# Layer 0's attention in float32 on half-array tiles of TensorE, in place of two fp32r parts

## The chip, the cores and the metric

The program runs on one core of one Trainium2 chip. The metric is the device time of one execution in microseconds (us). TensorE (PE) multiplies; VectorE (DVE), ScalarE (ACT) and GpSimd (POOL) do the rest on data in on-chip memory; SyncE (SP) issues most DMAs. An engine runs its own list of instructions in order. A `matmul` is a weight load (of the stationary operand, PEld in the profile) and a stream of the moving operand's columns (PE in the profile) into PSUM.

## The reference, cut to what matters

A two-layer transformer block on 512 latent tokens and 256 context tokens, width 1024, heads of 64. Layer 0's mixer is grouped attention, 4 query heads for each of 4 key/value heads: heads 0 and 1 (of the four) see the context and a window of 128 tokens to either side, with a sink; heads 2 and 3 see all tokens.

```python
qa = _rms(qa.reshape(b, n, HEADS_A, d), qn_a)      # the same for ka, qb, kb
qa, ka, qb, kb = _rope(qa, cos, sin), ...          # latent tokens only
...
s_c = jnp.einsum('bqhgd,bkhd->bhgqk', qb, k_ctx).astype(jnp.float32) * scale
s_w = jnp.einsum('bqhgd,bkhd->bhgqk', qb, kw).astype(jnp.float32) * scale
s_w = jnp.where(ok, s_w, NEG_INF)
p = _softmax(jnp.concatenate([s_c, s_w], axis=-1), sink_b).astype(v_lat.dtype)
return (jnp.einsum('bhgqk,bkhd->bqhgd', p[..., :n_ctx], v_ctx)
        + jnp.einsum('bhgqk,bkhd->bqhgd', p[..., n_ctx:], vw))
```

The output projection, a SwiGLU FFN, and layer 1 (differential attention, FFN) follow. All of it is float32.

## The kernel before

Tokens lie in 6 tiles of 128: tiles 0 to 3 are latent, 4 and 5 the context, which comes first in most loops (`CTX_FIRST`). A float32 product is made of fp32r ones: each operand is split into `hi` (a cast to fp32r) and `lo` (the rest), and three products are summed, or two where one operand's two parts lie side by side on the array.

Layer 0's mixer loops over the KV heads `b` = 0 to 3. The work of one `b` is the input projection of head `b` (`in_proj0`) and its attention (`attend0`); the projection of `b + 1` is written between the attention tiles of `b`, for `b` = 3 the output projection (`OutProj`) and the FFN's norm take that place. A dozen chunks of the modulations (`mod_chunk`) fill in too.

- `in_proj0`, for each token tile: 24 matmuls of 384 columns (`project`, L359 to L361), a copy out of PSUM (`qkv`, L421), the RMS norm and rotation of four q and one k (`qk_norm_rope`: squares on ACT, sum on DVE, the power -1/2 on POOL at L148, five to seven DVE products at L338 to L350), then the split of q into `qd` and of k into `kd` (ACT casts at L426, L430; the rest by DVE at L427 and POOL at L431), of v into `vv` (L422, L423), six PE transposes (L438, L444), and two ACT copies (L440, L445). A head's `qt` has hi and lo of its 64 rows on 128 partitions; `kT` has k's hi twice in one half and k's lo twice in the other.
- `attend0` for a token tile and a pair of heads (`hp`): for each head two matmuls of 256 columns against the context (L469, L470), two against the latent keys (L479, L480; 256, 384 or 512 columns) into one of **two** PSUM score tiles (`p_sc`, tag `sc`), masks by bf16 matmuls (L482); the maximum on DVE (L488, L492), the exponential with its sum on ACT (L493), which frees the score tile; 1 / sum, and the division of `Pt` by POOL (L502, L503). After a `yield`: `transposed_probs` (L386: PE transposes of 128x128, four to a PSUM bank; L372: ACT casts them to hi; L373: DVE subtracts for lo), then for each key tile two matmuls of 256 columns (L509, L510) into one `av`, whose halves of hi and lo of v are summed by two ACT copies and two DVE additions (L513 to L516).
- `Staggered` emits the first half of one pair before the second half of the one ahead of it.

The order on each engine is made by the framework's scheduler when the program is built: it takes instructions as their operands and buffers come free in its own timing, with the written order and `tc.high_priority` as preferences. What stands next to what on PE can therefore not be read from the code alone.

Of the kernel before, what the change touches and what calls it, by code (L numbers as in the profile page):

```python
# [18 lines left out]
P = 128  # L19
# [15 lines left out]
WBUF = 5  # places for units of an input projection's weights  # L35
PBUF = 4  # for probabilities
MODS0 = (0, 2, 2, 0)  # chunks of modulations beside layer 0's KV heads, by step
MODS1 = (2, 2, 2, 2, 2, 3, 3, 4, 4, 0)  # and beside layer 0's pairs of FFN tiles
# [18 lines left out]

def dram_rows(ap, n=P):
    """A row of DRAM, read into each of n partitions."""
# [4 lines left out]
def backbone(es: ExitStack, tc: tile.TileContext, x, c, ctx, c_ctx, mod_w, mod_b, norm_mix_w, norm_ffn_w,  # L64
# [28 lines left out]
    def acc_tile(name, n=512, one=None):  # L93
        """A bank to sum in: the given one of two, or each in turn."""
# [49 lines left out]
    def rsqrt(ss, n, inv, tag):  # L144
        """(ss * inv + EPS) ** -0.5, for n columns."""
# [6 lines left out]
    # modc[l][:, j, k, i]: column k of part j (shift, scale, gate of the mixer; the FFN's), stream i  # L152
# [3 lines left out]
    def mod_chunk(l, part, n, new_tile, pool, bank, wide=None, room=("modr", 1)):  # L156
        """Columns 256 * n ... of one of the six parts of layer l's modulation, four K-tiles side by side."""
# [23 lines left out]
    def mod_chunks_by_pool(chunks, pool):  # L181
        """Chunks, up to four streams of them, by GpSimd; the PE only sums over the partitions."""
        width = 256
        all_accs = []
        for l, part, n, streams in chunks:
            c0 = part * D + n * width
            accs = [pool.tile([P, width], F32, name="ma", tag="ma", bufs=4) for _ in range(streams)]
            for pc in range(2):
# [3 lines left out]
                for i, acc in reversed(list(enumerate(accs))):  # L192
                    # the first stream's products take the weights' place
# [11 lines left out]
        # the sums side by side on the PE's columns  # L205
# [4 lines left out]
        # the first sum's place is free now  # L210
# [11 lines left out]
    def add_mod(l, part, k0, k1, ps, streams):  # L222
        """Bias, and for a scale the factor that the norm's weight makes with it."""
# [8 lines left out]
    def gate_row(l, part, i, pool, bank=None):  # L232
        """Stream i's gate, on all partitions."""
# [4 lines left out]
        # by way of DRAM, as a row is to be on all partitions  # L238
# [19 lines left out]
    def cols_T(j, s0, s1):  # L258
        """Columns s0 to s1 of one of the two parts of h."""
# [34 lines left out]
    def unit(pool, views, shape, bufs, name, sub=None, new_tile=raw_tile):  # L294
        """Part of a weight, in two parts whose sum it is."""
# [16 lines left out]
    def rope_tables(pool, wq, wk):  # L312
        """cos and sin with the norm weights of q (and the scores' scale) and k; the weights alone for the context."""
# [14 lines left out]

    def qk_norm_rope(ps, nq, nk, t, w, tb, pool):
        """Heads of q (nq) and k (nk) from ps: RMS, weight, rotation, in token-major float32."""  # L330
# [22 lines left out]
    def project(ps, t, ws, c0, c1):  # L353
        """ps = h(t) @ W[:, c0:c1], W in units of two K-tiles."""
# [8 lines left out]
    def residual(xt, ps, g, n, pool=None, eng=nc.vector, rb=2):  # L363
        """Half n of xt += g * ps, by way of a tile of `pool` or in place."""
# [11 lines left out]
    def transposed_probs(Pt, heads, tiles, pool):  # L376
        """P's key tiles with the keys on the partitions, in two parts: [(hi, lo)] by key tile."""
# [637 lines left out]
```

## Time and profile before

| | |
|---|---|
| time, median of 3 runs | 1879.55 us (1876.51 to 1882.64) |
| profiled execution: first to last instruction | 1877.4 us, mean granted PE clock 0.982 |
| PE, PE weight loads busy | 1747.2 us, 1486.9 us |
| DVE, ACT, POOL busy | 1250.3, 762.4, 814.6 us |
| first and last matmul of layer 0's attention start | 71.7 us, 445.3 us |

The profiled execution has no time of its own in the list beside its span, which lies inside the runs' range, 2.2 us below their median. Engines are busy at the same time, so their busy times don't add up to the span; a matmul's end is modelled, with the way through the array in it, so that the distance from one start to the next is what a matmul costs in a stream. Line numbers in the text are those of this kernel (`before`) unless said otherwise. In the changed kernel the scores are at L507, masks L511, transposes of the probabilities L542, values L550, transposes of q and k L473.

### The profile page before, as it was taken

What the parts mean: (1) busy time and instruction counts of PE and PEld (TensorE: products, weight loads), DVE (VectorE), ACT (ScalarE), POOL (GpSimd) and SP (SyncE); (2) the same over time, 40 slices, a digit from 0 to 9 for tenths busy, and PEclk for the clock granted to TensorE, in tenths of its full rate; (3) what the DMA queues carried; (4) which work ended last, traced back from release to release, by engine and by line L of the source; (5) the groups of instructions that cost most, each with busy time, mean ns of one, the idle gap of its engine ahead of it and who ended that gap; (6) DMA issues with size and microseconds to landing.
All of it is one profiled execution on the core that took longest, in us unless ns stands there. A gap on an engine that the chain in (4) does not pass through costs nothing.

```text
span 1877.4 us, 26460 instructions
## 1 busy us (share of the span) xinstructions
PE 1747.2 (93%) x9910; PEld 1486.9 (79%) x9910; DVE 1250.3 (67%) x2103; ACT 762.4 (41%) x1618; POOL 814.6 (43%) x828
## 2 busy tenths in 40 slices
PE   6898989888999999999999889999997899999998
PEld 4887777666787888788888688999986688888887
DVE  4787777654448877667772658888877556566563
ACT  6567766643311122121111446767665323222220
POOL 2664654822079986736660555556543200000000
PEclk9999999999999999999999989999999999999999
DMA  9112322401543333423331121111103133223231
GB/s 311 40 42 65 105 68 68 126 22 56 168 136 101 102 101 123 140 81 114 117 122 59 64 70 57 35 34 42 47 12 124 45 104 110 90 90 113 68 111 46
DMA packets 152480, 165.66 MB, mean 88 GB/s; under 512 B 16480, under 2 KB 139936, under 8 KB 152352
## 3 DMA queue, kind: packets, MB, share of 16 engines
q1 hardware_dynamic: 152000, 163.77, 27.8%
q8 instruction: 78, 1.28, 0.3%
q14 instruction: 50, 0.41, 0.1%
q10 hardware_dynamic: 352, 0.21, 0.0%
HBM read 159.73 MB, written 4.22 MB: 87 GB/s over the span
## 4 chain that ended last, share of the span: by engine, by line
PE 68%; DVE 10%; POOL 7%; ACT 5%; issue 5%; DMA 4%; SPq 0%; POOLq 0%; ACTq 0%; DVEq 0%
PE pg L703 14%; PE pu L703 14%; PE dps L736 5%; PE dps L738 5%; PE dps L737 5%; PE inps L359 3%; PE inps L361 3%; PE inps L360 3%; PE ppt L386 2%; PE ops L670 2%; PE ops L672 2%; PE ops L671 2%; DMA modw<-in_mod_w_dram 1%; DMA wur<-in_ffn_w_in_dram 1%; DVE qz L347 1%
## 5 line engine op out<-in xcount | busy, mean ns | idle before, releaser
L703 PE MATMUL pg<-hT,wgh 128*128 128x512 f32 (+1 forms) x720 | 248.6, 394 | 5.2 <-ACT hT L287 5.2
L703 PE MATMUL pu<-hT,wuh 128*128 128x512 f32 (+1 forms) x720 | 243.4, 388 | 0.0
L366 DVE TENSOR_TENSOR rtmp<-dps,g 128x512 f32<-128x512 f32 x200 | 135.9, 687 | 160.9 <-PE dps L738 158.8
L367 DVE TENSOR_TENSOR x<-x,rtmp 128x512 f32<-128x512 f32 x188 | 202.0, 1082 | 3.8
L736 PE MATMUL dps<-wdh,hdh 128*128 128x512 f32 x440 | 177.1, 402 | 3.0 <-DVE rtmp L366 1.7
L737 PE MATMUL dps<-wdl,hdh 128*128 128x512 f32 x440 | 174.9, 398 | 0.0
L738 PE MATMUL dps<-wdh,hdl 128*128 128x512 f32 x440 | 172.2, 399 | 1.3 <-DVE hdl L373 1.2
L703 PEld LDWEIGHTS pg<-hT,wgh 128*128 128x128 f32 x720 | 136.6, 191 | 36.8 <-ACT hT L287 5.7
L703 PEld LDWEIGHTS pu<-hT,wuh 128*128 128x128 f32 x720 | 134.4, 188 | 29.7
L703 PE MATMUL pg<-hT,wgl 128*128 128x512 f32 (+1 forms) x360 | 141.7, 394 | 0.0
L703 PE MATMUL pu<-hT,wul 128*128 128x512 f32 (+1 forms) x360 | 139.6, 388 | 0.0
L372 ACT CAST hdh<-sg 128x768 fp32r<-128x768 f32 (+1 forms) x44 | 32.0, 728 | 258.0 <-DVE sg L718 257.9
L359 PE MATMUL inps<-wih,hT 128*128 128x384 f32 x384 | 132.6, 345 | 0.2 <-ACT qkv L557 0.2
L360 PE MATMUL inps<-wil,hT 128*128 128x384 f32 x384 | 130.6, 340 | 0.0
L361 PE MATMUL inps<-wih,hT 128*128 128x384 f32 x384 | 130.4, 340 | 0.0
L196 POOL TENSOR_TENSOR modw<-modw,cols 128x1024 f32<-128x1024 f32 x48 | 104.1, 2172 | 53.9 <-DMA modw<-in_mod_w_dram 53.6
L373 DVE TENSOR_TENSOR PTl<-ppt,PTh 128x512 fp32r<-128x512 f32 (+1 forms) x168 | 103.2, 619 | 14.0 <-ACT PTh L372 12.8
L372 ACT CAST PTh<-ppt 128x512 fp32r<-128x512 f32 (+1 forms) x168 | 88.4, 537 | 44.3 <-PE ppt L386 39.4
L736 PEld LDWEIGHTS dps<-wdh,hdh 128*128 128x128 f32 x440 | 82.9, 188 | 24.0 <-DVE rtmp L366 2.9
L738 PEld LDWEIGHTS dps<-wdh,hdl 128*128 128x128 f32 x440 | 83.1, 189 | 22.0 <-DVE hdl L373 2.1
L703 PE MATMUL pg<-hTc,wgh 128*128 128x256 f32 x352 | 98.2, 283 | 0.0
L703 PE MATMUL pu<-hTc,wuh 128*128 128x256 f32 x352 | 97.9, 282 | 0.0
(234 smaller groups left out, 4747.2 us busy)
## 6 DMA issues: line engine op xcount, KB each, us to landing
modw<-in_mod_w_dram SPq DMA_DIRECT2D x96, 512.0 KB, 4.4
wgr<-in_ffn_w_in_dram SPq DMA_DIRECT2D x44, 512.0 KB, 3.5
wur<-in_ffn_w_in_dram SPq DMA_DIRECT2D x44, 512.0 KB, 3.4
wdr<-in_ffn_w_out_dram SPq DMA_DIRECT2D x44, 512.0 KB, 3.5
wir<-in_od_w_in_dram SPq DMA_DIRECT2D x96, 128.0 KB, 2.3
x<-in_x_dram SPq DMA_DIRECT2D x8, 512.0 KB, 3.5
wir<-in_ev_w_in_dram SPq DMA_DIRECT2D x16, 256.0 KB, 2.8
wor<-in_ev_w_out_dram SPq DMA_DIRECT2D x8, 512.0 KB, 3.5
```

Source lines behind the costliest of these rows:

```text
L196: nc.gpsimd.tensor_tensor(pr, w, bc(sk, 2, width), ALU.mult)
L359: nc.tensor.matmul(ps, hs[0][:, k, :], a, start=k == 0, stop=False)
L360: nc.tensor.matmul(ps, hs[0][:, k, :], b, start=False, stop=False)
L361: nc.tensor.matmul(ps, hs[1][:, k, :], a, start=False, stop=k == KT - 1)
L366: nc.vector.tensor_mul(tmp, ps, g[:, n * 512:(n + 1) * 512])
L367: eng.tensor_add(xt[:, n * 512:(n + 1) * 512], xt[:, n * 512:(n + 1) * 512], tmp)
L372: nc.scalar.copy(hi, src)
L373: nc.vector.tensor_sub(lo, src, f32(hi))
L703: nc.tensor.matmul(ps[:, s0:s1], a, cols_T(b, s0, s1)[:, k, :], start=k == 0 and q == 0, stop=k == KT - 1 and q == 2)
L736: nc.tensor.matmul(ps, hh, a, start=j == 0, stop=False)
L737: nc.tensor.matmul(ps, hh, b, start=False, stop=False)
L738: nc.tensor.matmul(ps, hl, a, start=False, stop=j == nj - 1)
```

## The change

Scores and values of layer 0's attention become plain float32 matmuls, without parts.

- **Scores.** `qk` holds q of two heads on 128 partitions (64 rows each) and k twice. The two heads of a pair use rows 0 to 63 and 64 to 127 of the array: one matmul each for the context and for the latent keys, written in turns for the two heads.
- **Values.** All four heads of a `b` go together. For each key tile four transposes, one plain copy (ACT and DVE in turns), and two matmuls with v's 64 columns on columns 0 to 63 and 64 to 127 of the array. The result leaves PSUM by one ACT copy for the tile.
- **q and k.** The weights of the norm and the rotation come first, on the projection's copy (`rotate`), with tables that repeat for all five heads (`head_tables`). POOL multiplies by the norm's factor (L148's result) behind that, and copies v. Three float32 transposes and one ACT copy take the place of six and two.
- POOL's division of `Pt` becomes a `tensor_scalar`. `Pt` has 7 places (was 4). Emission is by tile, in three pieces.

```diff
     def tables0(j, tabs, wp):
-        tabs[j] = rope_tables(wp, *((ev_qn_a[0], ev_kn_a[0]) if j == 0 else (ev_qn_b[0], ev_kn_b[0])))
+        tabs[j] = head_tables(wp, *((ev_qn_a[0], ev_kn_a[0]) if j == 0 else (ev_qn_b[0], ev_kn_b[0])), 4, 1)
+    def rotate(raw, h0, n, t, wc, tb, pool):
+        sq = pool.tile([P, n * HD], F32, name="sq", tag="qz", bufs=2)
+        nc.scalar.activation(sq, raw, AF.Square)
+        ss = small.tile([P, n], F32, name="qss", tag="qss")
+        nc.vector.tensor_reduce(ss, sq.rearrange("p (h d) -> p h d", d=HD), AX.X, ALU.add)
+        r = rsqrt(ss, n, 1.0 / HD, "q")
...
+        nc.vector.tensor_tensor(z.rearrange("p h (a b) -> p (h a) b", b=2),
+                                swap_pairs(raw), tb[:, t, 1].rearrange("p h (a b) -> p (h a) b", b=2), ALU.mult)
+        nc.vector.tensor_tensor(y, rh, tb[:, t, 0], ALU.mult)
+        nc.vector.tensor_add(y, y, z)
+        return y, r
...
-            y = qk_norm_rope(raw, 4, 1, t, w, tb, wp)
-            qd = wp.tile([P, 4, 2, HD], F32R, name="qd", tag="qd", bufs=2)
-            nc.scalar.copy(qd[:, :, 0, :], y[:, 0:4])
-            nc.vector.tensor_sub(qd[:, :, 1, :], y[:, 0:4], f32(qd[:, :, 0, :]))
...
+            nc.gpsimd.tensor_copy(vv[:, t, :], raw[:, 320:384])
+            y, r = rotate(raw[:, 0:320], 0, 5, t, wc, tb, wp)
+            yn = wp.tile([P, 6, HD], F32, name="yn", tag="yn", bufs=2)
+            nc.gpsimd.tensor_tensor(yn[:, 0:4], y[:, 0:4], bc(r[:, 0:4], 2, HD), ALU.mult)
+            nc.gpsimd.tensor_scalar(yn[:, 4:6], bc(y[:, 4, :], 1, 2), r[:, 4:5], 1.0, ALU.mult, ALU.mult)
...
+                pt = tr_tile("qpt", [P, 3, P])
+                for h in range(3):
+                    nc.tensor.transpose(pt[:, h, :], yn[:, 2 * h:2 * h + 2].rearrange("p a d -> p (a d)"), ident)
+                nc.scalar.copy(qk[:, :, t * P:(t + 1) * P], pt)
...
-            nc.tensor.matmul(sc[:, 256:512], q, kT[:, 0, SEQ:TOK], start=True, stop=False)
-            nc.tensor.matmul(sc[:, 256:512], q, kT[:, 1, SEQ:TOK], start=False, stop=True)
...
+            scs = [p_sc.tile([P, 1024], F32, name="sc", tag="sc") for _ in range(2)]
+            rows = [slice(64 * hh, 64 * hh + 64) for hh in range(2)]
+            for s0, c0, c1, last in ((256, SEQ, TOK, True), (512, k0, k1, not masks))[:2 if nx else 1]:
+                for sc, rw in zip(scs, rows):
+                    nc.tensor.matmul(sc[:, s0:s0 + c1 - c0], qk[rw, hp, t * P:(t + 1) * P], qk[rw, 2, c0:c1],
+                                     start=True, stop=last)
...
-        PT = transposed_probs(Pt, 2, list(range(n // P)), mp)
-        av = acc_tile("av", 256, one=1)
-        for a, (hi, lo) in enumerate(PT):
-            v = vv[:, vt[a]].rearrange("p a d -> p (a d)")
-            nc.tensor.matmul(av, v, hi.rearrange("p h q -> p (h q)"), start=a == 0, stop=False)
-            nc.tensor.matmul(av, v, lo.rearrange("p h q -> p (h q)"), start=False, stop=a == len(PT) - 1)
...
+        for kc in range(nk):
+            pt = tr_tile("ppt", [P, 4, P])
+            for a, h in enumerate((0, 2, 1, 3)):
+                nc.tensor.transpose(pt[:, a, :], Pt[h][:, kc * P:(kc + 1) * P], ident)
+            PT = mp.tile([P, 4, P], F32, name="PT", tag="PT", bufs=4)
+            if kc % 2:
+                nc.vector.tensor_copy(PT, pt)
             else:
+                nc.scalar.copy(PT, pt)
+            for j in range(2):
+                nc.tensor.matmul(av[64 * j:64 * j + 64, :], vv[:, vt[kc], :],
+                                 PT[:, 2 * j:2 * j + 2].rearrange("p h q -> p (h q)"),
+                                 start=kc == 0, stop=kc == nk - 1)
+        nc.scalar.copy(o_t[t][:, 2 * b:2 * b + 2, :].rearrange("p k q -> p (k q)"), av)
```

What the scheduler makes of it on PE is seen at two places. The first is the scores of KV head 2, PE's order before. `sc_3788` and `sc_3795` are the score tiles of the two heads of a pair, `av` the values' sum, `kpt` a transpose of k.

```order
L469 MATMUL sc_3788<-kT_2060,qt_2959 128x256
L470 MATMUL sc_3788<-kT_2060,qt_2959 128x256
L479 MATMUL sc_3788<-kT_2060,qt_2959 128x512
L480 MATMUL sc_3788<-kT_2060,qt_2959 128x512
L509 MATMUL av_3638<-PTh_3634,vv_2061 128x256
L444 MATMUL kpt_3713<-identr_84,kd_3496 128x128 x2
L510 MATMUL av_3638<-PTl_3635,vv_2061 128x256
L509 MATMUL av_3638<-PTh_3634,vv_2061 128x256
L510 MATMUL av_3638<-PTl_3635,vv_2061 128x256
L469 MATMUL sc_3795<-kT_2060,qt_2959 128x256
```

The same kind of place in the changed kernel's order on PE, with the pair `sc_2977` (rows 0 to 63) and `sc_2978` (rows 64 to 127):

```order
L507 MATMUL sc_2977<-qk_1718 128x256
L507 MATMUL sc_2977<-qk_1718 128x512
L542 MATMUL ppt_3003<-cst_72,Pt_2879 128x128
L550 MATMUL av_2889<-PT_2904,vv_1719 64x256 x2
L542 MATMUL ppt_2994<-cst_72,Pt_2879 128x128
L171 MATMUL mod_2852<-modw_2853,s_pad_103 32x256 x4
L171 MATMUL mod_2852<-modw_2859,s_pad_103 32x256 x4
L507 MATMUL sc_2978<-qk_1718 128x256
L507 MATMUL sc_2978<-qk_1718 128x512
```

The two heads' scores, written in turns, stand apart: each head's two matmuls follow one another, with transposes, values and a modulation between the heads. Of the 160 score matmuls 30, in 15 pairs, stand directly beside one of the other half, so that the two can run at once.

The second place is the values, before: `ppt` are transposes of the probabilities, four to a bank, `PTh` and `PTl` the parts.

```order
L386 MATMUL ppt_3757<-cst_72,Pt_3589 128x128
L386 MATMUL ppt_3757<-cst_72,Pt_3590 128x128
L386 MATMUL ppt_3757<-cst_72,Pt_3589 128x128
L386 MATMUL ppt_3757<-cst_72,Pt_3590 128x128
L510 MATMUL av_3766<-PTl_3745,vv_2061 128x256
L509 MATMUL av_3766<-PTh_3744,vv_2061 128x256
L510 MATMUL av_3766<-PTl_3745,vv_2061 128x256
L509 MATMUL av_3766<-PTh_3753,vv_2061 128x256
```

And in the changed kernel, on PE, for token tile 0 of the same KV head:

```order
L550 MATMUL av_2993<-PT_2999,vv_1719 64x256 x2
L542 MATMUL ppt_3012<-cst_72,Pt_2879 128x128
L542 MATMUL ppt_3012<-cst_72,Pt_2917 128x128
L542 MATMUL ppt_3012<-cst_72,Pt_2882 128x128
L542 MATMUL ppt_3012<-cst_72,Pt_2920 128x128
L550 MATMUL av_2993<-PT_3008,vv_1719 64x256 x2
L542 MATMUL ppt_3021<-cst_72,Pt_2879 128x128
```

The values' two halves do stand side by side, and each such pair has whole-array transposes ahead of it and behind it. From the first score to the last value PE's order changes 350 times between instructions that use the whole array, half its rows, half its columns or a quarter of its columns (the modulations); before it is 32 times.

More of the change, by code (lines that the diff above doesn't have):

```diff
@@ L460, in attend0 @@
         n = CTX + nx * P
+        k0, k1 = xt0 * P, (xt0 + nx) * P
         vt = [4, 5] + list(range(xt0, xt0 + nx))
[L462 to L480 removed]
+        masks = []
@@ new lines, in attend0 @@
+        if isA and nx and t > 0:
+            masks.append((t - 1 - xt0, 0))
+        if isA and nx and t < NTX - 1:
+            masks.append((t + 1 - xt0, 1))
+        Pt = [None] * 4
+        for hp in range(2):
+            nm = small.tile([P, 2], F32, name="nm", tag="nm")
+            sm = small.tile([P, 2], F32, name="sm", tag="sm")
+            hs = 4 * b + 2 * hp
+            scs = [p_sc.tile([P, 1024], F32, name="sc", tag="sc") for _ in range(2)]
[4 more added lines that the diff above has]
+                                     start=True, stop=last)
+            for sc in scs:
@@ L752, in push, with step @@
             self.last = gen
+        def step(self):
+            next(self.last)
         def flush(self):
-            for _ in self.last:
+            for _ in self.last or ():
                 pass
-            self.last = ()
+            self.last = None
     def start_tile(shape, name):
```

145 lines of the change are left out of this document (69 added, 76 removed).

## The prediction

> **What bounds the kernel now.** First the page's head: PE is busy nearly all the time and makes up two thirds of the chain that ended last. That is an average over stages, so I go to the stage which the change touches, by the busy times in stretches, and set the middle of layer 1's mixer beside it, the nearest stage of the same build.
>
> ```profile
> PE 1747.2 (93%) x9910; PEld 1486.9 (79%) x9910; DVE 1250.3 (67%) x2103; ACT 762.4 (41%) x1618; POOL 814.6 (43%) x828
> PE 68%; DVE 10%; POOL 7%; ACT 5%; issue 5%; DMA 4%; SPq 0%; POOLq 0%; ACTq 0%; DVEq 0%
> ...
> core 0: us, PE busy (x) PEld busy (x) DVE busy (x) ACT busy (x) POOL busy (x), PEclk, DMA share, GB/s
> 72.00:445.00 373.00, 330.75 (x2199) 280.76 (x2198) 267.18 (x621) 232.22 (x600) 204.73 (x228) 0.99 0.23 69
> 1100.00:1350.00 250.00, 233.59 (x1588) 222.91 (x1587) 204.19 (x430) 163.73 (x447) 142.38 (x211) 0.98 0.15 43
> ```
>
> Layer 0's attention runs from 72 to 445 us. PE is idle there for 42 us of 373 (11%), in layer 1's stage for 16 of 250 (6.6%). DVE follows at 72%. So no engine alone bounds the stage: PE comes first and waits now and then. For whom, the waits of PE in this stretch say:
>
> ```profile
> PE sc L469 <- ACT Pt L493: 8.0, 12, 1.5
> PE ppt L386 <- DVE PTl L373: 5.9, 10, 1.2
> PE av L510 <- DVE PTl L373: 4.4, 10, 0.9
> PE av L509 <- DVE o L516: 4.3, 7, 0.9
> PE av L509 <- ACT PTh L372: 2.4, 3, 1.1
> ```
>
> They are the score tiles (freed by the exponential) and the split of the probabilities. Splitting goes away with the change, so PE's waits will shrink, and the question is what PE itself has to do. A busy share does not tell that, as a modelled end overlaps the next start. I take distances between starts, from PE's timeline (start, length, then the group):
>
> ```profile
> 202.47 0.33 PE L360 MATMUL inps<-wil,hT 128*128 128x384 f32 x1
> 202.64 0.34 PE L361 MATMUL inps<-wih,hT 128*128 128x384 f32 x1
> ...
> 299.97 0.60 PE L386 MATMUL ppt<-cst,Pt 128*128 128x128 f32 x4
> 300.50 1.07 PE L170 MATMUL mod<-modw,s_pad 128*32 128x256 f32 x16
> 301.50 0.66 PE L386 MATMUL ppt<-cst,Pt 128*128 128x128 f32 x4
> ...
> 303.99 0.28 PE L510 MATMUL av<-PTl,vv 128*128 128x256 f32 x1
> 304.11 0.28 PE L509 MATMUL av<-PTh,vv 128*128 128x256 f32 x1
> 304.23 0.28 PE L510 MATMUL av<-PTl,vv 128*128 128x256 f32 x1
> 304.35 0.60 PE L386 MATMUL ppt<-cst,Pt 128*128 128x128 f32 x4
> 304.88 0.64 PE L170 MATMUL mod<-modw,s_pad 128*32 128x256 f32 x8
> 305.45 0.38 PE L469 MATMUL sc<-kT,qt 128*128 128x256 f32 x1
> 305.68 0.28 PE L470 MATMUL sc<-kT,qt 128*128 128x256 f32 x1
> 305.79 0.39 PE L479 MATMUL sc<-kT,qt 128*128 128x512 f32 x1
> 306.02 0.39 PE L480 MATMUL sc<-kT,qt 128*128 128x512 f32 x1
> 306.25 0.28 PE L469 MATMUL sc<-kT,qt 128*128 128x256 f32 x1
> ```
>
> An fp32r matmul of 256 columns costs 0.12 us (303.99 to 304.11 to 304.23), of 512 columns 0.23 us (305.79 to 306.02), of 384 columns 0.17 us, a transpose 0.11 us (four take 0.60, the last 0.28 of it). With the counts of the loops the stage asks PE for: projection 426 x 0.174 = 74; probabilities' transposes 400 x 0.11 = 44; values 400 x 0.118 = 47; scores 224 x 0.118 + 32 x 0.175 + 64 x 0.232 = 47; output projection 216 x 0.232 = 50; modulations, masks and the small transposes about 30. Together 292 of 373 us. The other 81 us are waits and changes of the array's shape, which come next.
>
> **Scores and values as plain float32.** The modulations are the one plain float32 product in this trace.
>
> ```profile
> L170 PE MATMUL mod<-modw,s_pad 128*32 128x256 f32 x384 | 30.4, 418 | 2.8 <-DMA modw<-in_mod_w_dram 2.4 <-DVE modc L225 0.3
> ```
>
> 24 chunks of 8 matmuls give 384 records, so each matmul is two. They use a quarter of the array's columns each, and four go at once: 8 records (4 matmuls) took 0.64 us, 16 took 1.07, so four matmuls side by side add 0.43 us for 256 columns. A float32 matmul thus holds its part of the array 0.43 us per 256 columns, 0.65 for 384, 0.86 for 512.
>
> - **Values**: 200 matmuls of 256 columns on half the columns. The order has 93 pairs side by side and 14 alone: 107 x 0.43 = 46 us, against 47. No gain on PE.
> - **Scores**: 112 matmuls of 256 columns, 16 of 384, 32 of 512. One after the other: 112 x 0.43 + 16 x 0.65 + 32 x 0.86 = 86 us. All in pairs: 43 us. The order has only 15 pairs side by side, which save 7 us. The reason lies in the score tiles: there are two, the exponentials free them one after the other, and each head's matmuls are taken as soon as its own is free. So 79 us against 47: **+32 us**. Neither shape (64 rows, 64 columns) is in this trace; the ends are 43 us (as if all ran in pairs) and 86.
>
> **Changes of the array's shape.** Four transposes from 299.97 cost 0.44, to 300.41. The 16 records of L170 are four rounds of 0.215 = 0.86. The next transposes start at 301.50, and 0.06 of their 0.66 us is more than usual, so they run from 301.56: 1.15 us for 0.86 of streaming, 0.29 for two changes. From 304.35: free at 304.79, two rounds 0.43, and the scores from 305.45 with 0.38 in place of 0.28, that is 305.55: 0.33 for two. So **0.15 to 0.165 us a change**, 0.16 taken. The order has 350 changes in the stage, was 32: +318, **+51 us**, 56 in all where it was 5. If half arrays need none of this it is 0; if each costs the upper figure, 52. The Trainium skill, "TensorEngine Tiling (Array Packing)", Key Properties, says that a change of the tiling mode drains the engine, as opposed to a change of tile: a rule against this change. By it every one of the 350 costs, and the trace agrees for the quarter arrays with its 0.16 us; half arrays no run here shows yet.
>
> **What goes on the other engines.** Rows of the stretch 72 to 445 us:
>
> ```profile
> L373 DVE TENSOR_TENSOR PTl<-ppt,PTh 128x512 fp32r<-128x512 f32 x96 | 65.2, 685 | 9.3 <-ACT PTh L372 8.3
> L338 DVE TENSOR_TENSOR qy<-qkv,rs_q 128x320 f32<-128x320 f32 x20 | 14.9, 744 | 6.8 <-POOL rs_q L148 6.4 <-POOL kd L431 0.4
> L516 DVE TENSOR_TENSOR o<-av,otmp 64x128 f32<-64x128 f32 x47 | 13.9, 295 | 0.6
> L515 DVE TENSOR_TENSOR o<-av,otmp 64x128 f32<-64x128 f32 x47 | 13.0, 276 | 9.4 <-ACT otmp L514 9.3
> L427 DVE TENSOR_TENSOR qd<-qy,qd 128x256 fp32r<-128x256 f32 x20 | 11.5, 577 | 3.1 <-ACT qd L426 3.0
> L372 ACT CAST PTh<-ppt 128x512 fp32r<-128x512 f32 x96 | 55.5, 588 | 35.9 <-PE ppt L386 31.7 <-PE av L509 3.6
> L513 ACT COPY otmp<-av 64x128 f32<-64x128 f32 x47 | 12.4, 263 | 34.9 <-PE av L510 34.2
> L440 ACT CAST qt<-qpt 128x512 fp32r<-128x512 f32 x21 | 12.3, 588 | 2.5 <-PE qpt L438 2.5
> L431 POOL TENSOR_TENSOR kd<-qy,kd 128x128 fp32r<-128x128 f32 x21 | 10.3, 492 | 8.9 <-ACT kd L430 6.0 <-PE sc L470 2.2 <-POOL kd L431 0.5
> L503 POOL TENSOR_TENSOR Pt<-Pt,rc 128x256 f32<-128x256 f32 x16 | 12.0, 749 | 0.0
> ```
>
> DVE loses L373, L338, L515, L516 and L427, 118 us, and takes half of the 100 plain copies, some 50 x 0.69 = 34: from 267 to about 183. ACT gives back the other half of its casts (28 us) and most of the copies of L513 and L440: to about 160. POOL gains 0.75 + 0.49 us a tile (as L503 and L431) for the norm's factor, loses L431: some +13, to 218 of 373; a `tensor_scalar` for the division is not in the trace at such a size, and I take it as L503 (half or double would be -45 or +90 us of POOL, the second of which would make it the bound). Behind POOL's new products wait the transposes of q and k; they are needed one KV head later, and that distance hides them. The wider rotation tables cost DVE a few us once for each pair of KV heads, hidden by its idle quarter, or up to 3 us at the start if not. All this lies off PE, so it is worth only what it takes off PE's waits.
>
> **The sum.** PE is asked for 292 + 32 - 1 (values) - 3 (fewer small transposes) = 320 us, and 56 for changes: 376, where the stage had 373 in all. To this come PE's waits. With PE's list this full it is rarely empty; I take the idle share of layer 1's stage, 6.6% of some 400 us = 26, and let 2 us of the changes fall into waits. Bounds: 10 (nearly none) and 76 (81 less the 5 for changes: as now). 376 + 26 - 2 = 400 us, **+27 us** against 373. Before and behind the stage nothing that PE does changes: the count of its instructions in the FFNs and layer 1 is the same. The profiled span of 1877.4 becomes 1904; it lies 2.2 us below the median of the runs shown, so the time is **1907 us**.
>
> **Rivals.**
>
> - **Side by side after all.** If PE took a head's scores ahead of what stands between, the scores cost 43 us, not 79. The same page of the Trainium skill, under Theoretical Speedup, gives up to 2x for a dimension of 64 or less. By the rows: 376 - 36 = 340, with 26 to 45 of waits 366 to 385, so about 1882: no change. Against it: in all rows above PE starts in the order written, L510 behind L509. Chance 0.1.
> - **Rows for free.** If only changes of columns drain, the 145 changes between whole array and half rows cost nothing: -23 us, 1884, no change either. Only the quarter columns are in the trace, so it is open. Chance 0.09.
> - **The changes fall into waits: faster.** PE is idle for 42 us now, at just such places: a score that waits for its tile, a value that waits for its copy. If most changes happen while PE would wait anyway, changes and waits together come to some 30 us, not 80: 320 + 30 = 350, -23 us, 1857. It decides at 53 us for both (373 - 320): below it the change gains. Against it: the waits that the order can hide in are the ones that the lighter DVE and ACT remove, and the two changes priced above stand in a stream without waits. Chance 0.13.
> - **The waits stay.** A head's score now takes 1.29 us (0.43 + 0.86) instead of 0.70 between a free score tile and its maximum, so the circle of two tiles turns slower. If PE's waits stay at 76: 320 + 56 + 76 = 452, 1958. PE's longer list makes this unlikely as a whole, in part it is in my bounds. Chance 0.1.
>
> **Numbers.** The forecast has 0.58; with waits of 10 to 50 and changes of 45 to 56 us its own range is 1882 to 1933. A time within 0.3% (5.6 us) is about what a measurement can't tell from no change. Slower: 0.58 + 0.1 = 0.68; no change: most of 0.19, 0.17; faster: 0.13 and what is left, 0.15. For 8 times in 10 the range takes in half of the faster rival and of the slower one: 1866 to 1942.
>
> **What would show it.** In the changed profile: two records for each score and value, 0.215 us from one record to the next of 256 columns; a head's 768 columns in about 1.3 us; a gap of about 0.1 us ahead of the first matmul of another shape; PE's idle time in the stage below 42 us and DVE below 55% there. Wrong it would be if the two heads' score records overlap, if matmuls on half the rows follow without a gap, or if PE idles as long as before.

## The result, and the profile after

The changed kernel takes **1921.67 us** (median of four runs, 1916.96 to 1926.62) against 1881.1 us for the kernel before on the same chip (1876.51 to 1883.37): a ratio of 1.0224, 95% interval 1.0203 to 1.0245. It is slower, by some 41 us.

First the head of the page, from its busy times and from the chain that ended last.

```profile
PE 1820.6 (95%) x9838; PEld 1469.9 (76%) x9838; DVE 1152.9 (60%) x1871; ACT 697.2 (36%) x1398; POOL 778.5 (40%) x852
PE 74%; DVE 7%; POOL 7%; ACT 4%; DMA 4%; issue 3%; SPq 0%; POOLq 0%; ACTq 0%; DVEq 0%
```

DVE lost 97 us of work over the program, ACT 65, POOL 36; PE gained 73, and its share of the chain rose from 68% to 74%. So what was taken off the other engines came back on the one that sets the end. The stretches tell where: layer 0's attention, then FFN 0, then layer 1's mixer (columns as in the prediction).

```profile
74.70:474.00 399.30, 387.06 (x2115) 249.49 (x2114) 180.54 (x395) 171.07 (x396) 176.19 (x248) 0.97 0.20 63
500.00:1057.00 557.00, 539.07 (x2907) 453.82 (x2906) 358.67 (x380) 108.38 (x125) 330.96 (x226) 0.98 0.36 116
1057.50:1541.50 484.00, 439.10 (x2701) 399.63 (x2699) 347.87 (x721) 275.82 (x684) 234.63 (x326) 0.95 0.16 49
```

The attention takes 399.3 us, from its first score to its last value, where it took 373.5: +25.8. PE is idle there for 12 us (it was 42), and DVE's share went from 72% to 45%. The other two stretches were 551 and 472.7 us, though the change edits nothing in them: +6 and +11. PE's longest waits in the attention now:

```profile
PE sc L507 <- ACT Pt L524: 4.2, 5, 1.9
PE ppt L542 <- DVE nroom L285: 2.4, 2, 1.2
PE av L550 <- DVE PT L545: 1.2, 2, 0.8
```

The waits for the split of the probabilities (10.3 us) are gone. In their place stands this, from PE's timeline (start, length, group, number of records):

```profile
199.75 0.39 PE L550 MATMUL av<-PT,vv 128*64 128x256 f32 x2
200.07 1.07 PE L171 MATMUL mod<-modw,s_pad 128*32 128x256 f32 x16
201.07 0.33 PE L542 MATMUL ppt<-cst,Pt 128*128 128x128 f32 x1
201.33 1.34 PE L507 MATMUL sc<-qk 64*128 64x256 f32 x4
202.60 0.29 PE L511 MATMUL sc<-maskb,identb 128*128 128x128 bf16 x2
202.72 0.28 PE L542 MATMUL ppt<-cst,Pt 128*128 128x128 f32 x1
202.93 1.34 PE L507 MATMUL sc<-qk 64*128 64x256 f32 x4
204.20 0.28 PE L511 MATMUL sc<-maskb,identb 128*128 128x128 bf16 x2
```

One head's scores here are a matmul of 256 columns and one of 384, two records each (the row merges them under its first form), and hold PE from 201.33 to 202.60 = 1.27 us. As streams they would be 2 x 0.215 + 2 x 0.32 = 1.07: 0.20 lies in longer distances behind their first record and ahead of the mask. Another 0.15 lies ahead of them, where the transpose from 201.07 needs 0.11 and the scores start at 201.33. So the two changes of shape, on the way in and on the way out, cost some 0.35. The other head's scores come 1.6 us later, alone, with half of the array empty. Nothing waits here; PE is simply given more to do.

To see the whole stage in these terms I took the distances between the starts of all PE records in it and split each into the stream (0.12, 0.17, 0.23 us for an fp32r matmul of 256, 384, 512 columns, 0.215, 0.32 and 0.43 for a float32 record of 256, 384 and 512, 0.11 for a transpose; records side by side counted once), what a half-speed clock adds to that, and the rest. The rest ahead of a record of another shape, and behind the first record of a new shape, is put down to changes; all other rest is waits.

| stage, us | length | streams | half clock | changes (number) | waits |
|---|---|---|---|---|---|
| before | 373.5 | 290.5 | 4.9 | 7.4 (36) | 70.7 |
| after | 399.3 | 315.6 | 12.2 | 63.1 (349) | 8.4 |

By this rule a wait that ends ahead of another shape counts as a change. After has eight rests of over 0.4 us at such places, 5.8 us beyond the usual 0.1; without them a change costs 0.16 us in the stage and the waits are some 14 us. The waits of the table are also more than PE's idle time in the profile (42 us before), as a modelled end covers part of them.

### The profile page after: what moved, and what is told of

Read it like the earlier page. It is cut to its first block, busy times and chain, and to the rows that moved or that the text cites. A ratio compares the mean times of both kernels' runs of the same rounds, so it can differ in the third digit from the quotient of the medians.

```text
span 1924.2 us, 25733 instructions
## 1 busy us (share of the span) xinstructions
PE 1820.6 (95%) x9838; PEld 1469.9 (76%) x9838; DVE 1152.9 (60%) x1871; ACT 697.2 (36%) x1398; POOL 778.5 (40%) x852
## 4 chain that ended last, share of the span: by engine, by line
PE 74%; DVE 7%; POOL 7%; ACT 4%; DMA 4%; issue 3%; SPq 0%; POOLq 0%; ACTq 0%; DVEq 0%
PE pg L740 14%; PE pu L740 13%; PE sc L507 5%; PE dps L773 5%; PE dps L774 4%; PE dps L775 4%; PE inps L399 4%; PE inps L400 4%; PE inps L401 3%; PE av L550 3%; PE ppt L542 3%; PE ops L707 2%; PE ops L709 2%; PE ops L708 2%; DMA modw<-in_mod_w_dram 1%
## 5 line engine op out<-in xcount | busy, mean ns | idle before, releaser
L407 DVE TENSOR_TENSOR x<-x,rtmp 128x512 f32<-128x512 f32 x188 | 198.1, 1061 | 3.8
L197 POOL TENSOR_TENSOR modw<-modw,cols 128x1024 f32<-128x1024 f32 x48 | 98.1, 2047 | 56.8 <-DMA modw<-in_mod_w_dram 56.8
L507 PE MATMUL sc<-qk 64*128 64x256 f32 (+2 forms) x320 | 106.3, 480 | 4.3 <-ACT Pt L524 4.2
L534 POOL TENSOR_SCALAR Pt<-Pt,rc 128x256 f32<-128x256 f32 (+3 forms) x96 | 68.5, 727 | 85.4 <-DVE rc L531 71.2
```

The lines of the kernel that those rows point to most:

```text
L197: nc.gpsimd.tensor_tensor(pr, w, bc(sk, 2, width), ALU.mult)
L407: eng.tensor_add(xt[:, n * 512:(n + 1) * 512], xt[:, n * 512:(n + 1) * 512], tmp)
L507: nc.tensor.matmul(sc[:, s0:s0 + c1 - c0], qk[rw, hp, t * P:(t + 1) * P], qk[rw, 2, c0:c1], start=True, stop=last)
L534: nc.gpsimd.tensor_scalar(p[:, :n], p[:, :n], rc[:, hh:hh + 1], 1.0, ALU.mult, ALU.mult)
```

## The experiments

There are eleven runs, one of them the changed kernel unedited. The medians of the kernel before were 1879.6, 1880.9 and 1878.8 us in the three groups. Theory: the stage grew by scores that stream longer and by changes of shape at a full price, with waits that shrank to pay for part of it. Rivals: changes that cost little and a clock that does the rest; or a wait on GpSimd, which has the norm's factor now.

**The two halves of the change, one at a time.** First the new values with the scores, q and k as before (of the edit only the scores are shown; `Pt` has 6 places).

```diff
-                for sc, rw in zip(scs, rows):
-                    nc.tensor.matmul(sc[:, s0:s0 + c1 - c0], qk[rw, hp, t * P:(t + 1) * P], qk[rw, 2, c0:c1],
-                                     start=True, stop=last)
+                for hh, sc in enumerate(scs):
+                    for j in range(2):
+                        nc.tensor.matmul(sc[:, s0:s0 + c1 - c0], qs[t][:, 2 * hp + hh, :], kT[:, j, c0:c1],
+                                         start=j == 0, stop=last and j == 1)
...
```

> The values' part of the change alone: q, k path and scores as in the kernel before (fp32r in two parts), values plain float32 on half columns, all four heads together. Theory: scores 79 to 47 us, changes 349 to 206 (-21 us), small transposes +3, and 5 to 15 us more waiting because VectorE and ScalarE have the split of q and k again: 35 to 45 us below the changed kernel, about 1882 us, level with the kernel before. Rival (the loss is that of the values' half columns): no more than 10 us below the changed kernel, 1912 or more.

Measured: **1865.99 us**, 0.9927 of before (0.9912 to 0.9942), 14 us below it and 16 below the 1882 expected. Half of the change is a gain. The stage, from its row and by the same split:

```profile
71.60:425.70 354.10, 333.46 (x2181) 245.21 (x2180) 202.65 (x471) 187.07 (x459) 168.91 (x228) 1.00 0.23 71
```

354.1 us = 283.8 streams + 1.6 clock + 36.1 changes (208) + 32.6 waits. Against before the changes cost 29 us more and the waits 38 less. So the new values pay: they stream no longer than the two parts did, and PE waits less. That this is the spared split alone is not shown, as the cheaper division, the places of `Pt` and the emission by tile stay in this kernel too.

Then the other half, new scores, q and k with the values as before.

```diff
-            for j in range(2):
-                nc.tensor.matmul(av[64 * j:64 * j + 64, :], vv[:, vt[kc], :],
-                                 PT[:, 2 * j:2 * j + 2].rearrange("p h q -> p (h q)"),
-                                 start=kc == 0, stop=kc == nk - 1)
...
+            for a, (hi, lo) in enumerate(PT):
+                v = vv[:, vt[a]].rearrange("p a d -> p (a d)")
+                nc.tensor.matmul(av, v, hi.rearrange("p h q -> p (h q)"), start=a == 0, stop=False)
+                nc.tensor.matmul(av, v, lo.rearrange("p h q -> p (h q)"), start=False, stop=a == len(PT) - 1)
```

> The scores' part of the change alone: q, k path and scores as in the changed kernel, values as in the kernel before (split probabilities, fp32r, whole array). Theory: PE's streams as in the changed kernel, changes 349 to 196 (-23 us), but the split gives VectorE some 60 us and ScalarE some 50 us back, and with them 10 to 25 us of PE's waits: about 1917 us, between 1905 and 1930. Rival (the values' half columns make the loss): about 1882 us.

Measured: 1900.35 us, 1.0111 (1.0082 to 1.0139), below the 1905 to 1930 expected. Stage 390.6 = 317.1 streams + 7.5 clock + 40.3 changes (198) + 25.7 waits. The scores are the half that loses, and they lose it on PE: streams 27 us and changes 33 us longer than before, of which the waits give back 45, though the split of the probabilities is still there.

The two halves don't add up: -14 and +21 us alone, +41 together (in the stage -19, +17 and +26). Alone they shorten the 70.7 us of waits by 38 and by 45, together by only 62. Work that one half hides in waits finds those waits taken when the other half is there too.

**Scores on the whole array.** q gets zeros in the other head's rows; each matmul streams as long as the lone half did, but the shape stays that of the transposes.

```diff
-                for sc, rw in zip(scs, rows):
-                    nc.tensor.matmul(sc[:, s0:s0 + c1 - c0], qk[rw, hp, t * P:(t + 1) * P], qk[rw, 2, c0:c1],
+                for hh, sc in enumerate(scs):
+                    nc.tensor.matmul(sc[:, s0:s0 + c1 - c0], qk[:, 2 * hh + hp, t * P:(t + 1) * P], qk[:, 4, c0:c1],
```

> The changed kernel with the scores on the whole array, still plain float32: q stands in 128 rows of which the other head's 64 are zero, so that no change of shape goes with a score (changes 349 to 210 in the order), at the same stream time as a score that runs alone, 86 us against 79. Two more small ACT copies for each token tile. Theory (0.15 us a change): +7 - 21 = -14 us, about 1908 us. Rival (changes between whole array and half rows cost nothing): +7 us, about 1929.

Measured: **1894.4 us**, 1.0078 (1.0063 to 1.0093): 22 to 27 us below the changed kernel's two medians, where 14 were expected. The timeline shows a head's scores (256 and 384 columns again) shorter by the changes alone, and the stage's row a full clock:

```profile
200.76 1.24 PE L511 MATMUL sc<-qk 128*128 128x256 f32 x4
201.84 0.28 PE L515 MATMUL sc<-maskb,identb 128*128 128x128 bf16 x2
...
74.10:455.90 381.80, 363.98 (x2115) 251.01 (x2114) 180.76 (x397) 180.48 (x437) 179.31 (x249) 1.00 0.21 66
```

201.84 - 200.76 = 1.08 us for a head instead of 1.27. The stage is 17.5 us shorter than after: by the same split the changes take 28 us less (212 instead of 349) and half clock 10 less, while the streams take 6 more (no pair runs side by side) and the waits 15 more. The other 14 us between the two profiles lie in FFN 0 (8) and layer 1 (5), where nothing was edited. So in this order the half rows bring nothing: a matmul on 64 rows that runs alone takes as long as one on 128, and costs two changes more.

**The pair kept together.** The scheduler has to issue a pair's four matmuls as one block, so that the halves can run side by side.

```diff
-            for s0, c0, c1, last in ((256, SEQ, TOK, True), (512, k0, k1, not masks))[:2 if nx else 1]:
+            with tc.tile_critical():
+                for s0, c0, c1, last in ((256, SEQ, TOK, True), (512, k0, k1, not masks))[:2 if nx else 1]:
```

> The changed kernel with the score matmuls of a pair of heads kept together on PE (nothing may stand between them), so that the two halves of the array's rows run at once. Theory (scores one after the other cost 79 us of PE's list instead of 43, and each change of the array's shape 0.15 us): scores -36 us, changes 349 to 273 in the order, -11 us, and up to 20 us more waiting since a pair now needs both score tiles free: 25 to 45 us below the changed kernel, about 1885 us. Rival 1 (the halves don't overlap even when adjacent, only the changes count): -11 us, about 1910. Rival 2 (PE's list isn't the bound, the new work on GpSimd is): no difference, 1922.

Measured: **1995.1 us**, 1.0616 (1.0599 to 1.0633), far from all three expectations. Its timeline, its waits and the stage's row:

```profile
200.49 0.65 PE L551 MATMUL av<-PT,vv 128*64 128x256 f32 x4
201.95 0.70 PE L508 MATMUL sc<-qk 64*128 64x256 f32 x4 [0.81 <-DVE sm L530]
202.86 0.65 PE L551 MATMUL av<-PT,vv 128*64 128x256 f32 x4 [0.20 <-PEq L505]
...
PE sc L508 <- DMA modw<-in_mod_w_dram: 21.5, 6, 4.2
PE sc L508 <- DMA wor<-in_ev_w_out_dram: 8.2, 3, 4.8
PE sc L508 <- issue: 8.1, 10, 4.1
...
PE sc L508 <- DMA wir<-in_ev_w_in_dram: 3.8, 2, 3.3
...
90.40:560.00 469.60, 369.55 (x2062) 240.28 (x2064) 168.42 (x389) 165.42 (x388) 163.13 (x230) 0.87 0.16 51
```

Side by side it is: the four records from 201.95 are the 256 columns of both heads, two records at once each time, and the scores' streams of the stage (masks included) come to 45.6 us instead of 82.4. But PE's idle time is 100 of 469.6 us (70 of them ahead of L508), and the mean clock 0.87 (45 us lost to half clock). For 33.5 of the 70 us the profile names loads of weights that no score reads (`modw`, `wor`, `wir`) as what ended the wait; the exponential, which frees the score tiles, is named for none. That points at the block itself, but a wait for several things is put down to the last of them alone. To see whether its entry is what costs, it was made on PE alone.

```diff
-            with tc.tile_critical():
+            with tc.tile_critical(sync_engine=mybir.EngineType.PE, no_gpsimd_drain=True):
```

> The changed kernel with the score matmuls of a pair of heads kept together, as in e_pair, but with the section's entry tied to PE alone. Theory: the long waits of e_pair were those of the section's entry; without them scores take 45 us of PE's list instead of 82, changes of shape -76 x 0.15 = -11 us, and waiting for both score tiles costs up to 20: about 1890 us (1880 to 1905). Rival (waiting for two tiles at once is what costs, whatever the entry): near e_pair's 1995.

Measured: 1997.17 us, 1.0619 (1.0575 to 1.0662): no difference, near the 1995 of the rival, so the engine that does the entry isn't it. The exponential is named for none of the waits ahead of L508 here either. How much of the 70 us belongs to the two tiles, which a pair needs at once, and how much to the block as such stays open.

**Prices without waits.** Behind the changed kernel's last FFN stands a block of float32 matmuls of 256 columns whose results aren't used.

```diff
+        for _ in range(64):
+            nc.tensor.matmul(pa[:, 0:256], w, m, start=True, stop=True)
+        for _ in range(64):
+            nc.tensor.matmul(pa[:, 0:256], w[lo], m[lo], start=True, stop=True)
+        for _ in range(32):
+            nc.tensor.matmul(pb2[:, 0:256], w, m, start=True, stop=True)
+            nc.tensor.matmul(pa[:, 0:256], w[lo], m[lo], start=True, stop=True)
+        for _ in range(48):
+            nc.tensor.matmul(pa[:, 0:256], w[lo], m[lo], start=True, stop=True)
+            nc.tensor.matmul(pb2[:, 0:256], w[up], m[up], start=True, stop=True)
...
```

> The changed kernel with a block of plain float32 matmuls of 256 columns behind its last FFN, without waits between them, in six stretches: 64 on the whole array; 64 on rows 0 to 63 alone; 32 times one on the whole array and one on rows 0 to 63; 48 pairs on rows 0 to 63 and 64 to 127; 64 on columns 0 to 63 alone; 48 pairs on columns 0 to 63 and 64 to 127. The block's results aren't used. Time: the changed kernel's and some 165 to 200 us. Prices, all theories: 0.43 us a whole matmul, a lone half and a pair (27.5, 27.5, 20.6, 27.5, 20.6 us). Change of shape: with 0.1 us of gap and 0.05 of a longer first matmul the third stretch takes 64 x 0.58 = 37 us (at 0.16 each 37.8, without any price 27.5). Clock: if lone half rows as such make the clock fall (theory A), the second stretch has a granted clock of about 0.5 for most of its length and takes 40 to 55 us, the pairs stay at 1; then the fifth tells whether lone half columns do the same. If the half clock of the changed stage comes from short idle times alone (theory B), all stretches behind the first stay at 1.

Measured: one run, 2099.51 us. The stretches by time, behind the first 6 us (whole array; lone half rows; whole and half rows in turns; row pairs; lone half columns; column pairs):

```profile
1934.50:1959.20 24.70, 24.70 (x116) 21.57 (x114) 0.00 (x0) 0.00 (x0) 0.00 (x0) 1.00 0.00 0
1959.30:1987.10 27.80, 27.80 (x130) 23.85 (x129) 0.00 (x0) 0.00 (x0) 0.00 (x0) 1.00 0.00 1
1987.10:2026.60 39.50, 39.50 (x127) 18.65 (x126) 0.00 (x0) 0.00 (x0) 0.00 (x0) 1.00 0.00 0
2026.70:2047.90 21.20, 21.20 (x195) 19.56 (x194) 0.00 (x0) 0.00 (x0) 0.00 (x0) 1.00 0.01 2
2048.00:2075.20 27.20, 27.20 (x127) 17.29 (x127) 0.00 (x0) 0.00 (x0) 0.00 (x0) 1.00 0.00 1
2075.30:2096.30 21.00, 21.00 (x195) 16.01 (x193) 0.00 (x0) 0.00 (x0) 0.00 (x0) 1.00 0.00 1
```

And from the timeline of the third stretch:

```profile
1999.65 0.70 PE L1011 MATMUL pr<-x 128*128 128x256 f32 x2
2000.28 0.70 PE L1012 MATMUL pr<-x 64*128 64x256 f32 x2
2000.90 0.70 PE L1011 MATMUL pr<-x 128*128 128x256 f32 x2
```

A lone half costs 27.8 / 64 = 0.43 us, like a whole one; a pair 21.2 / 48 = 0.44, so side by side is a full factor of two. The third stretch has 64 matmuls and 64 changes in some 39.7 us, 12 more than without changes: **0.19 us a change**, for rows as well. (The rows above start 0.63 us apart, where a matmul alone takes 0.43.) And the clock stays at 1.00 through the lone halves: half rows as such don't slow it (theory A of this run falls).

**The clock.** The changed kernel once more, unedited, since its profiled run had 27 us at half clock in the stage where before had 10.

> The changed kernel once more, unedited, for its clock. In its first profile the granted clock stood at half for 27 us of the stage of layer 0's attention, 10 us in the kernel before, 3 us with the scores on the whole array or in fp32r. Theory (scores that fill half the rows let the clock gate fall): 15 us or more at half clock in the stage again, time 1915 to 1927. Rival (chance of the single profile): 3 to 10 us, and a time nearer to 1912.

Measured: 1916.89 us, 1.021 (1.0172 to 1.0249). Its profiled run has 20.5 us of half clock in the stage, as the theory had it, and a length of 398.6. Its four runs, 1914.24, 1915.85, 1917.94 and 1926.49 us, have mean clocks of 0.981, 0.978, 0.977 and 0.971: within a kernel the time goes with the clock, by some 10 us. Where it begins is seen in the first profile of after:

```profile
352.90:356.30 3.40, 3.40 (x23) 1.75 (x20) 2.93 (x5) 1.75 (x5) 3.28 (x3) 1.00 0.45 154
356.30:359.70 3.40, 2.83 (x9) 1.04 (x8) 1.02 (x2) 2.73 (x5) 3.17 (x3) 1.00 0.41 135
359.70:373.40 13.70, 13.70 (x42) 6.94 (x41) 4.80 (x8) 5.44 (x10) 8.20 (x6) 0.50 0.60 199
373.40:380.00 6.60, 6.60 (x38) 3.36 (x38) 1.81 (x3) 4.99 (x9) 3.83 (x3) 1.00 0.18 56
```

Two heads' scores with one idle time of 0.57 us between them, and the next 13.7 us run at half speed. Kernels with half-row scores had 17 to 27 us of half clock in the stage (after, a_again, e_oldvalues, e_normdve; e_divtt 13.7; e_pair and e_pair5, where PE idles most, over 120), those with whole-array scores 3.4 (e_full, e_fulldve, e_oldscores, e_best) or 10 (before). As lone halves in a stream keep the clock, half rows alone are not the cause; whether it takes the little waits as well, and which rule sets the clock, was not found out.

**Fewer changes.** To the faster half (new values, old scores): the values of two key tiles are taken together.

```diff
-        for kc in range(nk):
...
+        for kc0 in range(0, nk, 2):
+            PTs = []
+            for kc in (kc0, kc0 + 1):
...
+                PTs.insert(0, (kc, PT))
+            for i, (kc, PT) in enumerate(PTs):
+                for j in range(2):
+                    nc.tensor.matmul(av[64 * j:64 * j + 64, :], vv[:, vt[kc], :],
```

> e_oldscores with fewer changes of shape: the transposes of two key tiles first, then the value matmuls of both, the later one's ahead (changes 206 to 149 in the order, PE's streams the same). Theory (0.15 us a change): -8 us against e_oldscores, about 1857 us. Rival (changes that go away were covered by waits): no difference, 1866; if the longer way from transposes to values costs waits, 1870.

Measured: 1869.0 us, 0.994 (0.9919 to 0.996): no gain over 1865.99. In the stage the changes fell from 36.1 (208) to 27.8 us (152), the waits rose from 32.6 to 38.8, and the row of the score tiles shows where:

```profile
PE sc L519 <- ACT Pt L536: 10.0, 14, 2.9
72.70:423.40 350.70, 326.38 (x2180) 248.06 (x2178) 201.30 (x471) 185.59 (x459) 170.55 (x228) 1.00 0.24 73
```

It was 5.6 us, 7 times. Where PE has slack, a change less is mostly a wait more; the 3.4 us that the stage won went in layer 1 (486.9 us there against 480.3).

**GpSimd.** Three runs. The norm's factor on VectorE:

```diff
-            nc.gpsimd.tensor_tensor(yn[:, 0:4], y[:, 0:4], bc(r[:, 0:4], 2, HD), ALU.mult)
-            nc.gpsimd.tensor_scalar(yn[:, 4:6], bc(y[:, 4, :], 1, 2), r[:, 4:5], 1.0, ALU.mult, ALU.mult)
+            nc.vector.tensor_tensor(yn[:, 0:4], y[:, 0:4], bc(r[:, 0:4], 2, HD), ALU.mult)
+            nc.vector.tensor_scalar(yn[:, 4:6], bc(y[:, 4, :], 1, 2), r[:, 4:5], 1.0, ALU.mult, ALU.mult)
```

> The changed kernel with the norm's factor for q and k multiplied on VectorE instead of GpSimd. Theory (PE's list bounds the stage, both engines have room): within 5 us of the changed kernel, 1917 to 1927. Rival (GpSimd's longer list is what the projections' transposes wait for): 10 us or more below it.

Measured: 1903.96 us, 1.0143 (1.0106 to 1.0179): 13 to 18 us below after, which spoke for the rival. Its profile has 9 us of this in the stage (389.9), 6 in layer 1, where nothing was edited. If the factor's way over GpSimd were waited for, the gain had to come again with scores on the whole array. So the next kernel has both edits, these two lines and those of e_full.

> The changed kernel with two edits at once: scores on the whole array (zero rows), and the norm's factor on VectorE. Alone they gave 1894 and 1904 where the changed kernel has 1917 to 1922. If the factor's way over GpSimd costs PE waits of its own (theory), the gains add up: 1880 (1876 to 1886). If its gain came from the half rows' changes and clock that whole-array scores remove as well (rival), 1891 to 1896. If whole-array scores, having fewer changes, lay the waits for the factor bare, it is below 1876.

Measured: 1905.65 us, 1.0143 (1.0124 to 1.0163), above both expectations and 11 us above e_full. The stage differs by 1.5 us (380.3); the rest lies in FFN 0 (+8) and layer 1 (+5), untouched as they are. So with scores on the whole array the factor's place is worth 1.5 us in the stage, and e_normdve's gain is no proof of a wait. Where its 9 us in the stage come from stays open: the split puts some 4 of them on waits and 2 to 5 on half clock. Last, the division of the probabilities at the price that the prediction had for it:

```diff
-                nc.gpsimd.tensor_scalar(p[:, :n], p[:, :n], rc[:, hh:hh + 1], 1.0, ALU.mult, ALU.mult)
+                nc.gpsimd.tensor_tensor(p[:, :n], p[:, :n], rc[:, hh:hh + 1].to_broadcast([P, n]), ALU.mult)
```

> The changed kernel with GpSimd's division of the probabilities as a product of two tensors, as the prediction had priced it, in place of a product with a scalar per partition. GpSimd's 96 divisions get about twice as long, some 65 us more in the stage (245 of 400). If GpSimd's length is off the path there (as the prediction held): 1915 to 1927, no change. If the transposes of the probabilities wait for the division (rival, as the run with the factor on VectorE hints): half of the 0.7 us on 48 pairs, 1930 to 1950.

```profile
L534 POOL TENSOR_TENSOR Pt<-Pt,rc 128x768 f32<-128x768 f32 x32 | 46.3, 1471 | 26.5 <-DVE rc L531 15.9 <-DVE aff L230 10.0 <-PE mod L171 0.6
73.20:468.40 395.20, 378.86 (x2113) 245.44 (x2114) 184.86 (x395) 171.04 (x396) 210.26 (x247) 0.98 0.20 64
```

Measured: 1926.93 us, 1.0244 (1.0205 to 1.0283), no change within the runs' spread (1914.20 at a clock of 0.976, the others 1926 to 1928 at 0.968 to 0.971). GpSimd works 34 us more in the stage (65 were expected), and the stage is no longer for it: GpSimd is off the path there.

**What happens in layer 1.** No run was made for it, but the traces line up. PE's records there, some 2,700, can be compared by name, one after the other. Between before and after the two orders agree for 88%. In e_pair and e_pair5 PE's order is that of before (over 99%), in a_again, e_best, e_fulldve and e_divtt that of after (over 99%). One kernel of each, behind that of before:

```profile
1021.90:1494.60 472.70, 430.68 (x2702) 391.87 (x2700) 347.17 (x721) 275.71 (x684) 233.76 (x326) 0.97 0.16 50
```

```profile
1136.90:1610.90 474.00, 431.25 (x2702) 392.42 (x2700) 347.73 (x722) 276.26 (x684) 233.05 (x326) 0.97 0.16 50
```

```profile
997.90:1484.80 486.90, 437.97 (x2702) 398.79 (x2700) 348.84 (x722) 276.32 (x684) 234.10 (x326) 0.96 0.16 49
```

All with the first order take 473 to 474 us, all with the second 483 to 487, whatever layer 0 was like; a third (98% like after's, in e_full, e_oldscores, e_oldvalues, e_normdve) takes 477 to 480. It fits the 6 us of e_normdve and the 5 of e_fulldve as well. The counts are equal but for a few records. So the scheduler's order of layer 1 came out another way behind a changed layer 0, and 11 us go with it. That rests on twelve profiles that agree; no run changes this order alone. Part of the 11 us is half clock: 45 us of it in layer 1 in after and 38 in its second profile, 24.5 in before. It is not all, as e_pair5 has 35 and still the short time.

## Why the prediction was right or wrong

The forecast was 1907 us in a range of 1866 to 1942; 1921.67 lies inside, on the side that it gave most chance, with a growth of 41 us instead of 27. By its steps:

- **The stage**: 400 us forecast, 399.3 measured. The sum is right, its terms only in part; that they offset each other to within 1 us is luck.
- **Scores**: +32 us forecast (47 to 79); by PE's starts 49.5 to 82.4, with the masks in both, +33. The timeline shows the pair apart, as forecast. The reason given, score tiles that come free one after the other, is not shown by it. The exponentials that free the two tiles for the pair shown above do end one after the other, at 198.9 and 201.3 us (ACT, L524), but the first head starts at 201.33, when the second tile comes free as well. What keeps the heads apart in the run is the order, which is fixed when the program is built. e_pair shows that a pair kept together streams in half the time. **Values** as forecast (45.9 us against 46), and e_oldscores shows that this half of the change alone gains.
- **Changes of shape**: 0.16 us each for 350, 56 in all. Measured 0.18 each in the stage (63.1 / 349; 0.16 without the eight long rests) and 0.19 in the stream without waits. The term was about right. The rival of rows for free falls. The Trainium skill, "TensorEngine Tiling (Array Packing)", Key Properties, says that a change of tiling mode drains the engine; the runs agree for half rows and half columns too, in that each change costs. Its Theoretical Speedup, up to 2x for a dimension of 64 or less, is reached by the pairs of e_probe (0.44 us a pair, 0.43 a lone one); a half that runs alone gains nothing.
- **Waits**: 26 us less 2 forecast, 8.4 measured (14 with the eight long rests), 10 to 16 too many. This term was mis-sized: it was taken from the idle share of layer 1, and with its list full PE waits less than that. So the rival of waits that stay falls. That of changes which hide in waits needed 53 us for both; 63 + 8 = 71 is above it, however the long rests are counted. It does hold where PE has slack, as in e_best.
- **The clock**: not priced apart. Half clock took 12.2 us of streams in the stage in the first profile, 9.6 in the second, 4.9 before. So it filled about what the waits fell short of.
- **GpSimd**: +13 us forecast, with the division as a product of tensors; its stretch fell from 205 to 176. The form with a scalar is the cheaper one:

```profile
L534 POOL TENSOR_SCALAR Pt<-Pt,rc 128x768 f32<-128x768 f32 x32 | 28.6, 908 | 37.8 <-DVE rc L531 28.1 <-DVE modc L226 5.3 <-PE sc L507 4.4
```

  0.91 us for 768 columns, where e_divtt's form takes 1.47. It is off the path, so the miss cost nothing; DVE (181) and ACT (171) came out near the 183 and 160 forecast.
- **"Before and behind the stage nothing that PE does changes"**: this is the step that failed. The count of instructions is the same, as it said, but not their order. By the first profile the lead-in is 3 us longer, FFN 0 6.7 and layer 1 11.4; by the second 0.9, 1.6 and 11.0. With the stage's 25.8 and 25.1 that makes 47 and 39 us for the two profiled runs, on either side of the measured 41. In FFN 0 one wait stands out, for a chunk of the modulations, here before and after:

```profile
PE modcol L215 <- ACT ma L212: 4.9, 2, 4.5
```

```profile
PE modcol L216 <- ACT ma L213: 11.1, 2, 8.5
```

A version that beats both is e_oldscores, at 1866 us: the float32 values without the float32 scores.

## What to carry to other kernels

Half-array tiles are worth their price only where both halves of a pair stand next to each other in PE's order: look up the order before counting on the factor of two, and price every change of shape, since a half that runs alone costs as much as a whole one and up to two changes more. Split such a change into its halves, as one may gain and the other lose, but don't add their times up: both may count on the same waits. And where a scheduler makes the order, an edit in one stage may move the next ones by ten microseconds; read them as well, before a gain or a loss is put down to the edit.

## What the runs showed of the hardware

- A change between the whole array and half rows costs 0.19 us in a stream of float32 matmuls (e_probe: 64 changes, 12 us). In the mixed stage of after the median rest ahead of a new shape is 0.09 us, for half rows and half columns alike; behind its first record it is 0.10 for half rows and 0.05 for half columns.
- The granted clock is 1.00 or 0.50, in stretches of 3.4 us and its multiples (3.4, 6.8, 10.2, 13.7). The Trainium skill, "TensorE: Matmul & The Clock Gate", Part 1: The HAM clock gate, tells of a window of about 3.4 us, and of half speed after an idle one. The length agrees; the stretch from 359.7 us shown above had no idle window ahead of it, as PE was busy there for 2.83 of 3.40 us.
- GpSimd's product of 128x768 with a scalar per partition took 0.91 us (after), with a broadcast tensor 1.47 (e_divtt).
